# Half-by-half last units and a rearranged final LayerNorm in a two-block transformer kernel

## The chip, the cores and the metric

One core of a Trainium2 chip runs the whole program. The time is device microseconds of one execution, given as the median of several executions. The profile is one further execution, recorded by the hardware profiler; its times are counted from the start of its span.

## What is computed

The reference runs a token-mixing and feed-forward stack of two layers on a 512 x 1024 activation, and then one more block. That block ends with an expert layer, a residual and a LayerNorm, and only this end is touched here:

```python
x = layer_norm(DEEPNORM_ALPHA * x + f, ln2_g[l], ln2_b[l])      # f: the expert layer's output

def layer_norm(x, g, b):
    mu = jnp.mean(xf, axis=-1, keepdims=True)
    xc = xf - mu
    var = jnp.mean(xc * xc, axis=-1, keepdims=True)
    return xc * lax.rsqrt(var + LN_EPS) * g + b
```

The expert layer's second product is, over all 128 x 128 experts, (activation times gate) times the table v. For the last 384 of the 512 tokens it is done densely on TensorE, for the first 128 tokens by gathering the chosen rows of v.

## The kernel before, in words

The engines work as follows in the last stretch. A **unit** is one group of 128 experts: 128 x 1024 f32 numbers of v. `unit` (L253 to L262) loads it (DMA issued on SP, L257), rounds it to a high part `wh` on ScalarE (L260) and takes the rest `wl` on VectorE (L261); four raw buffers and three buffers each of `wh` and `wl` exist. `weighted` (L1884) also fetches the unit's activations, multiplies them by the gates (L1891) and splits them into `hi` and `lo` (`split`, L266 on ScalarE, L267 on VectorE). Products are made from high and low parts in three matmuls, (hi, wh), (lo, wh), (hi, wl), each into a PSUM bank of 128 tokens x 512 channels.

`second` (L1818) does this for one unit and one tile of 128 tokens `t`: three matmuls for each of the two channel halves m = 0 and 1, the halves in turn. There are three token tiles, so six PSUM banks `acc[2 * t + m]` sum up all units. For all units but the last five, `both` runs the three token tiles one after another, unit by unit: 18 matmuls a unit. The last five (`ENDS`) are held back as the list `ends`: the first two of them are split by halves into other buffers (`halves_in_blocks`), the other three use the three `wh` and `wl` buffers. They then run with the token tile as the outer loop, so that a tile's two banks are complete before the next tile begins: 30 matmuls a tile. After each tile `finish` is called.

`finish` (L1900) takes a tile of 128 tokens with 1024 channels. VectorE adds the residual, half by half, and sums each half (L1906); a one-column op makes minus the mean (L1909); ScalarE squares the row about the mean and sums it (L1911, with its accumulator read); VectorE makes the variance (L1912) and its reciprocal root by an integer estimate and three Newton steps (`rsqrt`, L325 to L331, nine one-column ops); one op makes mean times root (L1915). Then, for each half, ScalarE normalises (L1918), VectorE multiplies by the weight (L1919) and adds the bias (L1920), and SP issues the store (L1921). It is called four times: once for the gathered tile, ahead of `ends`, and once for each of the three dense tiles. Only its inputs differ.

**The order on each engine's queue** is not the order of the source. A planner of the framework goes through the program in its own estimated time and, each time an engine is free, takes the instruction that is ready and stands first in the source. An instruction whose input is not yet there lets one that stands later go ahead. Once planned, the order is fixed: on the chip each engine runs its queue in that order and waits where an input is late. The loads and splits of `ends` therefore stand among the instructions of the first `finish`.

Of the kernel before, what the change touches and what calls it, by code (L numbers as in the profile page):

```python
# [10 lines left out]
F32 = mybir.dt.float32  # L11
F32R = mybir.dt.float32r
BF = mybir.dt.bfloat16
I32 = mybir.dt.int32
U32 = mybir.dt.uint32
AF = mybir.ActivationFunctionType
OP = mybir.AluOpType
AX = mybir.AxisListType

P = 128  # L20
S = 512
D = 1024
# [8 lines left out]
LN_EPS = 1e-5  # L31
ALPHA = 2.0 ** 0.25
# [12 lines left out]
ROWS = 5  # L45
# [5 lines left out]
LEAD, ENDS = 7, 5  # L51
# [142 lines left out]
class Net:  # L194
# [1551 lines left out]
    def peer(self, out, begun):  # L1746
        nc, A = self.nc, self.A
        self.phase.close()
        self.stage = self.phase.enter_context(self.tc.tile_pool(name="stage", bufs=1))
        stage = self.stage  # L1750
# [12 lines left out]
        c0 = stage.tile([P, S], F32, name="c0", tag="c0")  # L1763
# [3 lines left out]
        XT = [self.cact] + [stage.tile([P, D], F32, name=f"xt{t}", tag=f"xt{t}") for t in range(1, NT)]  # L1767
        stats, heads = begun
        X, begun = [], [self.bank("proj") for _ in heads]
        for k, x in self.normed(stats, ln[:, 0], ln[:, 1], lambda k: self.x[k], self.t32):  # L1770
            X.append(self.new_pair())
            self.split(x, *X[k])
            c = slice(k * P, (k + 1) * P)
# [33 lines left out]
        def half(w, m):  # L1807
            return w[m] if isinstance(w, list) else w[:, m * S:(m + 1) * S]
# [6 lines left out]
                self.split(raw[:, m * S:(m + 1) * S], h[m], l[m])  # L1815
            return h, l

        def second(h, l, hi, lo, end, t):  # L1818
            for i, (a, w) in enumerate(((hi, h), (lo, h), (hi, l))):
                for m in range(2):  # L1820
                    q = 2 * t + m
                    nc.tensor.matmul(acc[q], lhsT=a[:, t * P:(t + 1) * P], rhs=half(w, m),  # L1822
                                     start=q not in started, stop=end and i == 2)
                    started.add(q)

        def both(args, end=False):
            for t in range(NT - early):
                second(*args, end, t)
# [23 lines left out]
        for j in range(kept, NE):  # L1852
# [6 lines left out]
            hi, lo = (v[:, :n] for v in self.new_pair())  # L1859
# [5 lines left out]
        row = [self.x[i] for i in range(4)]  # L1865
# [18 lines left out]
        def weighted(j, load=self.unit):  # L1884
            nonlocal fetched
            while fetched <= min(j + LEAD, 2 * j + 2):
                fetch(fetched)
                fetched += 1
            hs, g = coming.pop(0)
            w = load(A["pv"][:, j])  # L1890
            nc.vector.tensor_mul(hs, hs, g)  # L1891
            hi, lo = (v[:, :n] for v in self.new_pair())
            self.split(hs, hi, lo)
            return (*w, hi, lo)
# [4 lines left out]

        def finish(t, halves):  # L1900

            y = stage.tile([P, D], F32, name="row", tag="row", bufs=ROWS)
            parts, sq = self.sm(2, "fsum"), self.sm(2, "fsq")
            for m, v in enumerate(halves):
                c = slice(m * S, (m + 1) * S)
                nc.vector.scalar_tensor_tensor(y[:, c], XT[t][:, c], ALPHA, v, op0=OP.mult, op1=OP.add,  # L1906
                                               accum_out=parts[:, m:m + 1])
            mean, var = self.sm(1, "fmean"), self.sm(1, "fvar")
            nc.vector.scalar_tensor_tensor(mean, parts[:, :1], parts[:, 1:], self.negd, op0=OP.add, op1=OP.mult)  # L1909
            scr = stage.tile([P, D], F32, name="row", tag="row", bufs=ROWS)  # L1910
            nc.scalar.activation(scr, y, AF.Square, bias=mean, accum_out=sq[:, :1])  # L1911
            nc.vector.tensor_scalar(var, sq[:, :1], 1.0 / D, LN_EPS, op0=OP.mult, op1=OP.add)  # L1912
            r = self.rsqrt(var, 1)
            mr = self.sm(1, "fmr")
            nc.vector.tensor_mul(mr, mean, r)  # L1915
            for m in range(2):
                c = slice(m * S, (m + 1) * S)
                nc.scalar.activation(y[:, c], y[:, c], AF.Identity, scale=r, bias=mr)  # L1918
                nc.vector.tensor_mul(y[:, c], y[:, c], row[m])  # L1919
                nc.vector.tensor_add(y[:, c], y[:, c], row[2 + m])  # L1920
                nc.sync.dma_start(out[t * P:(t + 1) * P, c], y[:, c])  # L1921

        self.negd = self.sm(1, "negd", bufs=1)
        nc.vector.memset(self.negd, -1.0 / D)
        for j in range(kept - ENDS):
            both(weighted(j) if j else first)
            if not self.gathered:
                gather(ROW_STEPS[3])
                if self.gathered:
                    finish(0, [vacc[:, :S], vacc[:, S:]])  # L1930
        if not self.gathered:
            for _ in rows:
                pass
            finish(0, [vacc[:, :S], vacc[:, S:]])
        ends = [weighted(kept - ENDS + i, halves_in_blocks if i < ENDS - 3 else self.unit) for i in range(ENDS)]
        for t in range(NT - early):
            for i, e in enumerate(ends):
                second(*e, i == ENDS - 1, t)
            finish(early + t, acc[2 * t:2 * t + 2])


# [47 lines left out]
```

## Time and profile before

| what | us |
|---|---|
| median of 3 runs | 3672.79 |
| lowest and highest of them | 3670.61 and 3675.13 |
| the profiled execution, its own time | 3671.99 |
| the span of its profile | 3670.2 |

The span reaches from the first to the last instruction; the 1.8 us between it and the execution's own time lie around it. PE is TensorE's matmuls, PEld its weight loads, DVE is VectorE, ACT ScalarE, POOL GpSimd; SP issues DMAs. TensorE's granted clock is given as a share: 1.00 is 2.4 GHz, 0.50 is 1.2 GHz. A row of the timeline has start, duration, engine, line, operation, output and inputs, shapes and count; in brackets the idle time of the engine ahead of it and what ended that.

### The profile page before, as it was taken

The page shows a single profiled execution, that of the slowest core. Times are in us where ns is not written, and L with a number is a line of the kernel's source. Part 1 is how long each engine was busy: PE and PEld are TensorE (multiplying, and loading weights), DVE is VectorE, ACT ScalarE, POOL GpSimd, SP SyncE. Part 2 cuts the span into 40 slices and gives each one's busy share as a digit, 9 for nine tenths or more (in the row PEclk, how much of TensorE's full clock was granted, in tenths as well). Part 3 has the DMA queues.
Part 4 walks back from the last instruction along what each step waited for, and adds up shares of the span by engine and source line. Part 5 has one row for each costly group of instructions (what it writes and reads, how often), then busy time and mean ns, then how long its engine had stood idle before and what let it go on. Part 6 is the DMA issues. An engine that isn't in the chain of part 4 may idle for free. (4 is left out here: it accounts for less than half of the span.)

```text
span 3670.2 us, 49271 instructions
## 1 busy us (share of the span) xinstructions
PE 3554.5 (97%) x18265; PEld 3019.0 (82%) x18265; DVE 2394.7 (65%) x4791; ACT 1562.9 (43%) x2769; POOL 369.2 (10%) x358
## 2 busy tenths in 40 slices
PE   7999999999999999999999999899899999999998
PEld 6888876788888888767888887788899999988786
DVE  6555687665563334776533386699877667778787
ACT  4332366433233323465432263433667753334333
POOL 0000100000000001000000000021221134432220
PEclk9999999999999999999999999999999999999999
DMA  7666320266653333401333322265686879999995
GB/s 249 190 186 198 115 94 18 64 202 193 201 178 109 94 95 105 133 24 31 91 98 93 97 79 68 84 202 195 206 289 235 296 262 308 313 327 346 336 341 183
DMA packets 259665, 635.72 MB, mean 173 GB/s; under 512 B 82336, under 2 KB 117584, under 8 KB 256864
## 3 DMA queue, kind: packets, MB, share of 16 engines
q1 hardware_dynamic: 206368, 473.96, 40.1%
q0 software_dynamic: 39808, 140.52, 11.2%
q10 hardware_dynamic: 13248, 18.09, 1.3%
q8 instruction: 143, 2.34, 0.3%
q14 instruction: 98, 0.80, 0.1%
HBM read 591.32 MB, written 41.16 MB: 172 GB/s over the span
## 5 line engine op out<-in xcount | busy, mean ns | idle before, releaser
L260 ACT ACTIVATE wh<-raw 128x1024 fp32r<-128x1024 f32 (+2 forms) x620 | 645.3, 1043 | 1129.3 <-PE proj L283 880.6
L261 DVE TENSOR_TENSOR wl<-raw,wh 128x1024 fp32r<-128x1024 f32 (+2 forms) x620 | 744.1, 1201 | 508.4 <-ACT wh L260 370.1
L283 PE MATMUL proj<-yh,wh 128*128 128x512 f32 (+1 forms) x2744 | 644.7, 375 | 9.1 <-ACT hg L1839 4.2
L283 PE MATMUL proj<-yh,wl 128*128 128x512 f32 (+1 forms) x2744 | 629.1, 371 | 13.6 <-DVE wl L261 13.6
L283 PE MATMUL proj<-yl,wh 128*128 128x512 f32 (+1 forms) x2744 | 628.4, 370 | 0.0
L283 PEld LDWEIGHTS proj<-yh,wl 128*128 128x128 f32 x2744 | 506.4, 189 | 82.8 <-DVE wl L261 15.5
L283 PEld LDWEIGHTS proj<-yh,wh 128*128 128x128 f32 x2744 | 501.1, 189 | 85.0 <-ACT hg L1839 5.7
L283 PEld LDWEIGHTS proj<-yl,wh 128*128 128x128 f32 x2744 | 505.4, 189 | 67.5
L535 DVE SCALAR_TENSOR_TENSOR scr<-raw,cact 128x1024 bf16<-128x1024 f32 x128 | 156.7, 1224 | 136.3 <-DMA raw<-in_wada 136.0
L1822 PE MATMUL acc<-wl,yh 128*128 128x512 f32 x756 | 236.2, 394 | 2.7 <-DVE wl L261 2.6
L1822 PE MATMUL acc<-wh,yh 128*128 128x512 f32 x756 | 235.0, 392 | 3.6 <-ACT yh L266 2.1
L1822 PE MATMUL acc<-wh,yl 128*128 128x512 f32 x756 | 234.3, 391 | 0.3 <-DVE yl L267 0.3
L1737 POOL DMA_INDIRECT row<-in_purows,c x128 | 156.5, 1223 | 537.9 <-DVE row L1721 261.6
L667 DVE TENSOR_TENSOR ga<-sg,proj 128x512 f32<-128x512 f32 x88 | 60.5, 687 | 225.7 <-PE proj L283 223.2
L1737 POOL DMA_INDIRECT row<-in_pv,c x128 | 165.2, 1291 | 392.6 <-DVE vacc L1729 275.8
L272 PE MATMUL proj<-yl,wh 128*128 128x256 f32 (+1 forms) x552 | 177.0, 330 | 10.6 <-DVE yl L394 7.0
L273 PE MATMUL proj<-yh,wl 128*128 128x256 f32 (+1 forms) x552 | 174.6, 324 | 2.2 <-DVE wl L261 2.2
L1822 PEld LDWEIGHTS acc<-wl,yh 128*128 128x128 f32 x756 | 141.1, 188 | 38.4 <-DVE wl L261 9.5
L271 PE MATMUL proj<-yh,wh 128*128 128x256 f32 (+1 forms) x552 | 164.8, 328 | 7.8 <-ACT yh L640 6.3
L1822 PEld LDWEIGHTS acc<-wh,yh 128*128 128x128 f32 x756 | 142.1, 189 | 32.0 <-ACT yh L266 2.5
L1822 PEld LDWEIGHTS acc<-wh,yl 128*128 128x128 f32 x756 | 142.5, 189 | 31.4 <-DVE yl L267 1.0
L1729 DVE SCALAR_TENSOR_TENSOR vacc<-row,act,vacc 128x1024 f32<-128x1024 f32 x127 | 162.5, 1280 | 0.6
(465 smaller groups left out, 5166.7 us busy)
## 6 DMA issues: line engine op xcount, KB each, us to landing
raw<-in_wada SPq DMA_DIRECT2D x144, 512.0 KB
raw<-in_pu SPq DMA_DIRECT2D x128, 512.0 KB
raw<-in_pv SPq DMA_DIRECT2D x128, 512.0 KB
raw<-in_wg SPq DMA_DIRECT2D x84, 512.0 KB
raw<-in_wu SPq DMA_DIRECT2D x84, 512.0 KB
raw<-in_wd SPq DMA_DIRECT2D x64, 512.0 KB
gates<-st SPq DMA_DIRECT2D x20, 1024.0 KB
acts<-hg ACTq DMA_DIRECT2D x92, 192.0 KB
```

The source lines that it names most:

```text
L260: nc.scalar.activation(h[:, :n], raw[:, :n], AF.Copy)
L261: self.latest = nc.vector.tensor_sub(l[:, :n], raw[:, :n], h[:, :n].bitcast(F32)).ins
L271: mm(out, lhsT=lh, rhs=rh, start=start, stop=False)
L272: mm(out, lhsT=lh, rhs=rl, start=False, stop=False)
L273: mm(out, lhsT=ll, rhs=rh, start=False, stop=stop)
L283: self.nc.tensor.matmul(ps, lhsT=w[:, k * P:(k + 1) * P], rhs=X[c + k][part], start=c + k + i == 0, stop=i == 2 and c + k == nk - 1)
L535: nc.vector.scalar_tensor_tensor(scr, raw, 1.0, self.cact, op0=OP.mult, op1=OP.mult, accum_out=self.mod[:, l, j:j + 1])
L667: nc.vector.tensor_mul(a, sg, p[1])
L1729: nc.vector.scalar_tensor_tensor(acc, row, a, acc, op0=OP.mult, op1=OP.add)
L1737: nc.gpsimd.indirect_dma_start(out=row, out_offset=None, in_=tables[kind], in_offset=bass.IndirectOffsetOnAxis(ap=self.experts[:GT, s:s + ...
L1822: nc.tensor.matmul(acc[q], lhsT=a[:, t * P:(t + 1) * P], rhs=half(w, m), start=q not in started, stop=end and i == 2)
```

## The change

In the loop over the last five units the channel half becomes an outer loop: for each token tile first all five units for half 0 (15 matmuls), then all five for half 1. `second` gets the halves as an argument; `both` still runs both.

In `finish`, each half of the row is squared by itself as soon as it is there, about minus the mean of the first half (`c0`), with a bf16 scratch as the output that is not used. The difference `off` between the full mean and `c0` corrects the variance afterwards. VectorE subtracts the mean and multiplies by the weight into a second row buffer `z`, ahead of the root; after the root one op for each half multiplies by the root and adds the bias. ScalarE's normalising pass and the product of mean and root are gone. The stores are as before.

```diff
--- before.py
+++ after.py
@@ -1815,9 +1815,9 @@
                 self.split(raw[:, m * S:(m + 1) * S], h[m], l[m])
             return h, l
 
-        def second(h, l, hi, lo, end, t):
+        def second(h, l, hi, lo, end, t, halves=range(2)):
             for i, (a, w) in enumerate(((hi, h), (lo, h), (hi, l))):
-                for m in range(2):
+                for m in halves:
                     q = 2 * t + m
                     nc.tensor.matmul(acc[q], lhsT=a[:, t * P:(t + 1) * P], rhs=half(w, m),
                                      start=q not in started, stop=end and i == 2)
@@ -1899,26 +1899,31 @@
 
         def finish(t, halves):
 
+
             y = stage.tile([P, D], F32, name="row", tag="row", bufs=ROWS)
+            z = stage.tile([P, D], F32, name="row", tag="row", bufs=ROWS)
+            scr = self.tmp.tile([P, D], BF, name="scr", tag="scr", bufs=1)
             parts, sq = self.sm(2, "fsum"), self.sm(2, "fsq")
+            c0, mean, var, off = (self.sm(1, v) for v in ("fc0", "fmean", "fvar", "foff"))
+            cs = [slice(m * S, (m + 1) * S) for m in range(2)]
             for m, v in enumerate(halves):
-                c = slice(m * S, (m + 1) * S)
-                nc.vector.scalar_tensor_tensor(y[:, c], XT[t][:, c], ALPHA, v, op0=OP.mult, op1=OP.add,
+                nc.vector.scalar_tensor_tensor(y[:, cs[m]], XT[t][:, cs[m]], ALPHA, v, op0=OP.mult, op1=OP.add,
                                                accum_out=parts[:, m:m + 1])
-            mean, var = self.sm(1, "fmean"), self.sm(1, "fvar")
+                if m == 0:
+                    nc.vector.tensor_scalar(c0, parts[:, :1], -1.0 / S, None, op0=OP.mult)
+                nc.scalar.activation(scr[:, cs[m]], y[:, cs[m]], AF.Square, bias=c0, accum_out=sq[:, m:m + 1])
+
             nc.vector.scalar_tensor_tensor(mean, parts[:, :1], parts[:, 1:], self.negd, op0=OP.add, op1=OP.mult)
-            scr = stage.tile([P, D], F32, name="row", tag="row", bufs=ROWS)
-            nc.scalar.activation(scr, y, AF.Square, bias=mean, accum_out=sq[:, :1])
-            nc.vector.tensor_scalar(var, sq[:, :1], 1.0 / D, LN_EPS, op0=OP.mult, op1=OP.add)
+            nc.vector.tensor_scalar(off, mean, c0, None, op0=OP.subtract)
+            for m in range(2):
+                nc.vector.scalar_tensor_tensor(z[:, cs[m]], y[:, cs[m]], mean, row[m], op0=OP.add, op1=OP.mult)
+            nc.vector.tensor_scalar(off, off, off, -LN_EPS, op0=OP.mult, op1=OP.add)
+            nc.vector.tensor_scalar(var, sq[:, :1], sq[:, 1:], 1.0 / D, op0=OP.add, op1=OP.mult)
+            nc.vector.tensor_scalar(var, var, off, None, op0=OP.subtract)
             r = self.rsqrt(var, 1)
-            mr = self.sm(1, "fmr")
-            nc.vector.tensor_mul(mr, mean, r)
             for m in range(2):
-                c = slice(m * S, (m + 1) * S)
-                nc.scalar.activation(y[:, c], y[:, c], AF.Identity, scale=r, bias=mr)
-                nc.vector.tensor_mul(y[:, c], y[:, c], row[m])
-                nc.vector.tensor_add(y[:, c], y[:, c], row[2 + m])
-                nc.sync.dma_start(out[t * P:(t + 1) * P, c], y[:, c])
+                nc.vector.scalar_tensor_tensor(z[:, cs[m]], z[:, cs[m]], r, row[2 + m], op0=OP.mult, op1=OP.add)
+                nc.sync.dma_start(out[t * P:(t + 1) * P, cs[m]], z[:, cs[m]])
 
         self.negd = self.sm(1, "negd", bufs=1)
         nc.vector.memset(self.negd, -1.0 / D)
@@ -1934,8 +1939,9 @@
             finish(0, [vacc[:, :S], vacc[:, S:]])
         ends = [weighted(kept - ENDS + i, halves_in_blocks if i < ENDS - 3 else self.unit) for i in range(ENDS)]
         for t in range(NT - early):
-            for i, e in enumerate(ends):
-                second(*e, i == ENDS - 1, t)
+            for m in range(2):
+                for i, e in enumerate(ends):
+                    second(*e, i == ENDS - 1, t, [m])
             finish(early + t, acc[2 * t:2 * t + 2])
```

## Rows read from the trace of the kernel before

**Rows 1.** The page, part 1: busy time and share of the span, by engine.

```profile
PE 3554.5 (97%) x18265; PEld 3019.0 (82%) x18265; DVE 2394.7 (65%) x4791; ACT 1562.9 (43%) x2769; POOL 369.2 (10%) x358
```

**Rows 2.** The chain of work that ended last: start, us, what; its last piece.

```profile
3666.42 0.69 DVE row L1920
```

**Rows 3.** Busy time by stretch: tiles 1, 2, 3, and the end (clock, DMA share last).

```profile
3632.58:3641.77 9.19, 7.38 (x31) 5.47 (x30) 7.80 (x20) 4.47 (x7) 0.00 (x0) 1.00 0.07 29
3641.77:3648.59 6.82, 6.82 (x31) 5.63 (x30) 4.22 (x17) 2.67 (x4) 0.00 (x0) 1.00 0.10 38
3648.59:3655.60 7.01, 6.96 (x31) 5.44 (x29) 5.35 (x19) 1.33 (x3) 0.00 (x0) 1.00 0.19 75
3655.60:3670.20 14.60, 0.00 (x0) 0.00 (x0) 8.86 (x26) 4.28 (x6) 0.00 (x0) 0.64 0.19 72
```

**Rows 4.** Timeline of VectorE over the last tile's `finish`.

```profile
3655.83 0.69 DVE L1906 SCALAR_TENSOR_TENSOR row<-xt,acc 128x512 f32<-128x512 f32 x1
...
3656.44 0.68 DVE L1906 SCALAR_TENSOR_TENSOR row<-xt,acc 128x512 f32<-128x512 f32 x1
...
3657.05 1.29 DVE L1919 TENSOR_TENSOR row<-row,x 128x512 f32<-128x512 f32 x2
...
3659.46 0.21 DVE L1909 SCALAR_TENSOR_TENSOR fmean<-fsum,negd 128x1 f32<-128x1 f32 x1
3660.98 0.15 DVE L1912 TENSOR_SCALAR fvar<-fsq 128x1 f32<-128x1 f32 x1 [1.31 <-ACT row L1911]
3661.17 0.15 DVE L325 TENSOR_SCALAR rsg<-fvar 128x1 int32<-128x1 int32 x1
...
3663.28 0.16 DVE L1915 TENSOR_TENSOR fmr<-fmean,rsy 128x1 f32<-128x1 f32 x1
3664.37 0.69 DVE L1919 TENSOR_TENSOR row<-row,x 128x512 f32<-128x512 f32 x1 [0.93 <-ACT row L1918]
```

**Rows 5.** Timeline around the last units: VectorE, then ScalarE, then TensorE.

```profile
3629.97 0.69 DVE L1906 SCALAR_TENSOR_TENSOR row<-cact,vacc 128x512 f32<-128x512 f32 x1
...
3631.86 1.21 DVE L267 TENSOR_TENSOR yl<-hs,yh 128x384 fp32r<-128x384 f32 x2
...
3634.66 1.22 DVE L261 TENSOR_TENSOR wl<-raw,wh 128x1024 fp32r<-128x1024 f32 x1
...
3639.33 0.69 DVE L1919 TENSOR_TENSOR row<-row,x 128x512 f32<-128x512 f32 x1
3639.93 1.22 DVE L261 TENSOR_TENSOR wl<-raw,wh 128x1024 fp32r<-128x1024 f32 x1
...
3633.54 1.04 ACT L260 ACTIVATE wh<-raw 128x1024 fp32r<-128x1024 f32 x1
3637.14 1.52 ACT L1918 ACTIVATE row<-row,fmr,rsy 128x512 f32<-128x512 f32 x2 [2.56 <-issue]
3638.57 1.04 ACT L260 ACTIVATE wh<-raw 128x1024 fp32r<-128x1024 f32 x1
...
3639.66 0.74 PE L1822 MATMUL acc<-wh,yh 128*128 128x512 f32 x2 [1.49 <-ACT wh L260]
...
3641.20 0.73 PE L1822 MATMUL acc<-wl,yh 128*128 128x512 f32 x2 [0.33 <-DVE wl L261]
```

**Rows 6.** Groups by line and shape over the whole span: two kinds of VectorE op.

```profile
L1161 DVE SCALAR_TENSOR_TENSOR p<-p,w 128x512 f32<-128x512 f32 x8 | 6.0, 745 | 0.0
...
L330 DVE TENSOR_SCALAR rst<-rsy,fvar 128x1 f32<-128x1 f32 x12 | 3.3, 272 | 0.4
```

**Rows 7.** Busy time by stretch, columns as in rows 3: clock around earlier TensorE gaps.

```profile
2932.44:2934.46 2.02, 0.01 (x2) 0.01 (x1) 1.81 (x4) 1.56 (x4) 1.34 (x1) 1.00 0.70 251
...
2935.93:2939.34 3.41, 3.41 (x12) 3.41 (x11) 2.25 (x4) 3.23 (x9) 1.14 (x1) 0.50 0.96 338
...
2594.61:2604.85 10.24, 9.03 (x27) 8.53 (x28) 10.24 (x58) 3.09 (x4) 2.34 (x2) 0.50 0.66 206
```

## Prediction

> **What bounds the kernel now.** I read the page first: TensorE is busy 97% of the span, VectorE 65% [rows 1]. So only what makes TensorE wait, or what comes after its last matmul, can show. The change touches nothing ahead of the first `finish` and the last five units, about the last 41 us of 3670. Next I read the chain that ended last: it is `finish` of the last tile [rows 2]. Then the stretches [rows 3]: each begins with a tile's first matmul. Tile 2 is 30 matmuls in 6.82 us, 0.227 us each, with the PE column full; tile 1 takes 9.19 us, so TensorE waits about 2.4 us in it or at its edges; after 3655.60 there are 14.60 us without a matmul. These two, the wait in tile 1 and the tail, are what the change can move. 0.2% of this time is 7.3 us, which is about what a measurement of this kernel can tell from no change.
>
> **The tail, and VectorE's work per tile.** From the last tile's second L1906 (3656.44) to the last L1920's end (3666.42 + 0.69 = 3667.11) pass 10.7 us [rows 2, 4]. Three parts of that are not needed: 2.4 us (3657.05 to 3659.46) in which VectorE still finishes the tile before, 1.31 us of waiting for the full-row square, and 1.1 us from the product of mean and root (3663.28) to the first L1919 (3664.37), ScalarE's normalising pass [rows 4]. Both ScalarE round trips leave the chain.
>
> VectorE pays for it. Before, a tile costs it two L1906 at 0.61, L1909 0.25, L1912 0.19, the root 2.1 (3661.17 to 3663.28), the product 0.2 and four row ops at 0.61 to 0.67: 6.6 us [rows 4]. After: two L1906 1.2; `c0` 0.2; the mean 0.25; `off` 0.25; two products (y + mean) * weight; the correction 0.2; two variance ops 0.5; the root 2.1; two ops that scale and add the bias. The four row ops now take a column as scalar; the nearest such row, L1161, takes 0.745 us against 0.69 [rows 4, 6], so I take a pitch of 0.67, 2.7 us for four. Sum **7.4 us a tile**. The five new one-column ops aren't in the trace. They lie between a pitch of 0.07, as if fully overlapped, and 0.3 for a Newton step's op with two column scalars (0.272 busy, L330 [rows 6]); I take 0.2 to 0.25 as most of them have one such operand. The ends give 6.8 and 7.8 us a tile.
>
> 7.4 is more than the 6.82 us in which TensorE makes a tile, so VectorE sets the pace of the last three tiles. Let T be the end of tile 1's matmuls. Its second half is taken up some 0.3 us later (L1906 follows the last matmul by at most that [rows 3, 4]). What is left of tile 1 is 7.4 less a first L1906 and `c0`: 6.6. Two more tiles are 14.8. The end is T + 0.3 + 6.6 + 14.8 = T + 21.7. Before, T is 3641.77 and the end 3667.11: T + 25.3. **The tail gives 3.6 us.** The first half's early sum and square (ScalarE, two half rows and two reads instead of one row and one) are covered by the row products; a full-row square and read make VectorE wait 1.31 [rows 4], so this is the cost of a half at most, were that cover gone. The first `finish` works on gathered rows alone and gains nothing by halves, but it gets the same longer VectorE list. The last stores still take 3.1 us from 3667.11 to the span's end; their issue moves from 1.3 us apart to 0.7, worth nothing to 0.6 us later, and I take nothing.
>
> **The wait for the last unit.** This decides the sign. Before, tile 1 runs 24 matmuls, both halves of four units, before it asks for the fifth unit; there it waits 1.49 us for `wh` and 0.33 us for `wl` [rows 5]. That `wh` stands on ScalarE behind the two L1918 of the first `finish` (3637.14), which wait for its root. Those leave the queue, so `wh` can follow the one at 3633.54 and be done by about 3635.6. But `wl` is VectorE's, and there L261 stands behind the same `finish` (3639.33, then 3639.93). After the change, half 0 asks for the last unit after only 12 matmuls. Tile 1 begins at 3632.58, so this is 3635.3, and `wl` is wanted two matmuls later, at 3635.8.
>
> Where will L261 stand? The planner prefers what stands first in the source. `finish` comes first; L261 only slips into a gap where a one-column op waits for the one before. One of the two splits sits in such a gap (3634.66), the last one (3639.93) came only behind the root and most row ops [rows 5]. I take the same for after. The queue from 3629.97 on is: L1906 0.7, `c0` 0.2, L261 1.2, mean 0.2, two L267 1.2, `off` 0.2, two products 1.3, three one-column ops 0.7, L267 0.5, L261 1.2, root 2.1, two last row ops 1.3, and then the last L261 1.2: 12.0 us, so `wl` is there at **3642.0** (3641.2 before). TensorE then still owes 16 matmuls of tile 1 instead of two: 3.6 us, T = 3645.6, **3.9 us later** (3641.77 before).
>
> With L261 ahead of the two last row ops it would be 2.5 later. The other bound is L261 straight behind its `wh`, 3635.6 + 1.2 = 3636.8: a wait of 1.0, and T = 3632.58 + 6.82 + 1.0 = 3640.4, 1.3 us earlier than before.
>
> **The clock.** A wait of about 6 us (3635.8 to 3642.0, less a few matmuls) is longer than any TensorE had in this stretch. Its clock stayed at 1.00 over the 1.5 us wait [rows 3, 5]. Elsewhere, after a gap of 2.0 us, the granted clock stood at 0.50, which is 1.2 GHz, for the next 3.41 us; the longest such stretch that I read, 10.24 us, followed a longer gap [rows 7]. At 0.50 half of the stretch is lost. Nothing to 5.1 us are the bounds; I take one short stretch, **1.7 us**, as part of it can fall into the wait itself.
>
> **Sum:** 3.9 + 1.7 - 3.6 = +2.0 us on the profiled execution's 3671.99, which is 3674.0. That execution lies 0.8 under the median of the runs; the runs spread over 4.5 us, so I leave it there. It is no measurable change.
>
> VectorE is at 65% of the span and at 4.22 of 6.82 us in tile 2 [rows 1, 3], so it looks far from full. The Trainium skill says in "Perfetto Trace Analysis", Optimizing Scalar/DVE Operations, that where these engines aren't saturated but cause bubbles elsewhere, breaking up instructions may let work complete sooner. By that rule TensorE's pace would hold; my row-by-row sum says that the change itself fills VectorE. The rule's case is the second rival.
>
> **The rivals.**
> - The planner puts the last L261 early (into a gap of the root, say). For it: one split sits in such a gap, and ScalarE is free sooner. Against: the last unit's buffers come free late, and `finish` got longer on VectorE. With the early bound, -1.3 - 3.6 = -4.9: 3667.1, no clock loss. In between, L261 ahead of the last two row ops: 2.5 + 1.0 - 3.6, about 3672.
> - VectorE keeps up, and the tiles run at TensorE's pace. The end is T + 13.6 + 0.3 + 6.6 = T + 20.5, 1.1 us sooner than I say: 3672.9. It needs under 6.8 us a tile, the low end above.
> - Slower: the wait at the last unit drops the clock for long. With 10.24 us at half, 3.9 + 5.1 - 3.6 = +5.4: 3677.4. It would pass 0.2% from a half-clock stretch of 14 us on, and no row shows one with TensorE at work. If the clock stayed low over all 76 matmuls left, that is the case.
> - The halves do nothing: VectorE is behind anyway when half 0 is complete, so its early sum buys no time. This is within my sum, as VectorE sets the pace there.
>
> **Chances.** My forecast 0.5 (3671 to 3677); early L261 0.25; TensorE's pace 0.15; long half clock 0.1, a half of it beyond 0.2%. A gain of over 7.3 us needs the early split, TensorE's pace and more at once: 0.05. So faster 0.05, same 0.89, slower 0.06. The range reaches from the early split's 3667.0 to the long half clock's 3677.5.
>
> **What would show it.** Right: in tile 1 a TensorE wait on L261 of 3 us or more, after 12 to 15 matmuls; a clock of 0.50 behind it; VectorE without gaps from tile 1's end on; the end some 21.7 us after tile 1's. Wrong: the last L261 ahead of the root's end, tile 1 in under 9 us, or VectorE idle ahead of the last tile's second L1906.

## The result, and the profile after

The changed kernel takes **3716.37 us** (median of 5 runs, 3712.79 to 3728.95) against 3673.16 (5 runs) before: ratio **1.0122** with a 95% interval of 1.0104 to 1.0140. The forecast was 3674.0 and no measurable change; the kernel is 43 us slower than before. The profiled execution is the slowest of the five, 3728.95, with a span of 3727.1, so its times lie 57 us over before's span rather than 43.

First the page of the changed kernel: the span and part 1, to be read against [rows 1].

```profile
span 3727.1 us, 49271 instructions
...
PE 3613.8 (97%) x18265; PEld 3027.7 (81%) x18265; DVE 2396.4 (64%) x4803; ACT 1559.4 (42%) x2769; POOL 370.5 (10%) x358
```

TensorE runs the same 18265 matmuls and is still busy 97% of the span, but 59.3 us longer in sum (3613.8 against 3554.5). This is a little more than the difference of the spans (56.9). The time went into the matmuls themselves, not into waits.

Next, where in the span it went. The first matmul of the last five units is a fixed event: the change has no instruction of TensorE ahead of it. It starts at 3632.58 before [rows 3] and at 3689.52 after, 56.9 us later. From there to the end of the span pass 37.6 us before (3670.20 - 3632.58) and 37.6 us after (3727.10 - 3689.52). **All of the loss arises ahead of the code that was changed.** With the n-th matmul of one trace beside the n-th of the other, the lag is 3 us at 186 us, 14 at 860, 30 at 1450 and 47 at 2400. It is still 47 at 3000, and 57 from 3450 on. So it does not arise at one place: it grows where matmuls of 512 columns run (750 to 900 us hold 662 of them and add 4.4 us, 0.0066 each) and stands still where there are few (340 of the 3373 matmuls from 2400 to 3000).

Then one stretch in the middle. The timeline of TensorE of the kernel before, 800 to 806 us; a row is a run of matmuls with its start and duration:

```profile
800.57 1.98 PE L283 MATMUL proj<-yh,wh 128*128 128x512 f32 x8
802.38 1.98 PE L283 MATMUL proj<-yl,wh 128*128 128x512 f32 x8
804.20 1.98 PE L283 MATMUL proj<-yh,wl 128*128 128x512 f32 x8
```

and the same of the changed kernel:

```profile
800.08 2.03 PE L283 MATMUL proj<-yh,wl 128*128 128x512 f32 x8
801.95 2.03 PE L283 MATMUL proj<-yh,wh 128*128 128x512 f32 x8
803.82 2.03 PE L283 MATMUL proj<-yl,wh 128*128 128x512 f32 x8
```

From start to start, eight matmuls take 1.815 us before (half of 804.20 - 800.57) and 1.87 after: a pitch of 0.227 and of 0.234 us. No row has a wait in brackets. The same comes out of windows over 60 us (window, us, PE busy and count, granted clock, DMA share, GB/s), first of the kernel before, then of the changed one:

```profile
800.00:860.00 60.00, 60.00 (x267) 1.00 0.63 196
```

```profile
800.00:860.00 60.00, 60.00 (x259) 1.00 0.63 190
```

TensorE has no gap and its clock is at 1.00, which is 2.4 GHz, but it makes 259 matmuls in a time in which the kernel before makes 267. Neither a late input nor the clock explains that: the same instruction is 3% slower. Lines L283 and L1822 alone have 7008 and 2304 matmuls of 512 columns; 9312 times 0.0066 us would be 61 us. Not all of that shows: from 3450 to 3600 us 642 of them run and the lag does not grow. There the kernel before itself waits 1.7 us for inputs, with a DMA share of 1.01.

**The last 38 us went much as forecast.** The stretches of the changed kernel, tiles 1, 2, 3 and the end (columns as in [rows 3]), and, as the last row, the stretch behind tile 1's wait:

```profile
3689.52:3703.30 13.78, 9.89 (x31) 7.24 (x30) 8.17 (x23) 2.61 (x5) 0.00 (x0) 0.75 0.11 39
3703.30:3710.26 6.96, 6.96 (x31) 5.63 (x30) 6.41 (x23) 1.63 (x4) 0.00 (x0) 1.00 0.00 0
3710.26:3717.40 7.14, 7.12 (x31) 5.45 (x29) 6.79 (x24) 1.63 (x4) 0.00 (x0) 1.00 0.20 75
3717.40:3727.10 9.70, 0.00 (x0) 0.00 (x0) 6.19 (x21) 0.81 (x2) 0.00 (x0) 0.60 0.29 108
...
3697.15:3702.00 4.85, 4.85 (x11) 3.79 (x12) 0.85 (x3) 0.81 (x2) 0.00 (x0) 0.50 0.09 32
```

Tile 1 takes 13.78 us instead of 9.19, and the end without matmuls 9.70 instead of 14.60. TensorE's timeline has the wait in brackets:

```profile
3692.79 0.47 PE L1822 MATMUL acc<-wh,yl 128*128 128x512 f32 x1
3697.15 0.80 PE L1822 MATMUL acc<-wl,yh 128*128 128x512 f32 x1 [3.88 <-DVE wl L261]
3697.74 0.63 PE L1822 MATMUL acc<-yh 128*128 128x512 f32 x1
```

After 14 matmuls TensorE waits 3.88 us for the last `wl`, and comes back at a granted clock of 0.50. VectorE's timeline says why, and what pace the tiles have:

```profile
3690.12 0.21 DVE L1920 TENSOR_SCALAR foff<-foff 128x1 f32<-128x1 f32 x1
3690.25 0.20 DVE L1921 TENSOR_SCALAR fvar<-fsq 128x1 f32<-128x1 f32 x1
...
3694.54 1.41 DVE L1925 SCALAR_TENSOR_TENSOR row<-row,rsy,x 128x512 f32<-128x512 f32 x2
3695.87 1.22 DVE L261 TENSOR_TENSOR wl<-raw,wh 128x1024 fp32r<-128x1024 f32 x1
...
3703.50 0.69 DVE L1910 SCALAR_TENSOR_TENSOR row<-xt,acc 128x512 f32<-128x512 f32 x1 [4.64 <-PE acc L1822]
...
3710.47 0.68 DVE L1910 SCALAR_TENSOR_TENSOR row<-xt,acc 128x512 f32<-128x512 f32 x1
...
3717.44 0.68 DVE L1910 SCALAR_TENSOR_TENSOR row<-xt,acc 128x512 f32<-128x512 f32 x1
...
3722.60 1.42 DVE L1925 SCALAR_TENSOR_TENSOR row<-row,rsy,x 128x512 f32<-128x512 f32 x2
```

The last split stands behind the root and both last row ops (L1925) of the first `finish`, and each tile's second half (L1910, before L1906) follows the one before by 6.97 us. The first two rows are new one-column ops; they start 0.13 us apart.

### The profile page after: what moved, and what is told of

Read it like the earlier page. It is cut to its first block, busy times and chain, and to the rows that moved or that the text cites. A ratio compares the mean times of both kernels' runs of the same rounds, so it can differ in the third digit from the quotient of the medians.

```text
span 3727.1 us, 49271 instructions
## 1 busy us (share of the span) xinstructions
PE 3613.8 (97%) x18265; PEld 3027.7 (81%) x18265; DVE 2396.4 (64%) x4803; ACT 1559.4 (42%) x2769; POOL 370.5 (10%) x358
## 4 chain that ended last, share of the span: by engine, by line
PE 82%; DVE 11%; DMA 3%; ACT 2%; issue 1%; SPq 0%; ACTq 0%; DVEq 0%
PE proj L283 52%; PE acc L1822 13%; PE proj L272 2%; PE proj L273 2%; PE proj L271 2%; DVE wl L261 2%; PE gp L1690 2%; PE o L1091 1%; PE tp L869 1%; PE sc L809 1%; DMA gates<-st 1%; PE pnat L271 1%; PE pnat L272 1%; PE pnat L273 1%; DVE ch L1343 1%
## 5 line engine op out<-in xcount | busy, mean ns | idle before, releaser
L261 DVE TENSOR_TENSOR wl<-raw,wh 128x1024 fp32r<-128x1024 f32 (+2 forms) x620 | 744.1, 1201 | 549.1 <-ACT wh L260 419.2
L283 PE MATMUL proj<-yh,wh 128*128 128x512 f32 (+1 forms) x2744 | 653.6, 378 | 8.5 <-ACT hg L1839 4.0
L283 PE MATMUL proj<-yh,wl 128*128 128x512 f32 (+1 forms) x2744 | 641.3, 376 | 12.6 <-DVE wl L261 12.6
L283 PE MATMUL proj<-yl,wh 128*128 128x512 f32 (+1 forms) x2744 | 640.3, 375 | 0.0
L283 PEld LDWEIGHTS proj<-yh,wl 128*128 128x128 f32 x2744 | 507.6, 189 | 92.4 <-DVE wl L261 14.8
L283 PEld LDWEIGHTS proj<-yh,wh 128*128 128x128 f32 x2744 | 500.5, 189 | 93.9 <-ACT hg L1839 5.5
L283 PEld LDWEIGHTS proj<-yl,wh 128*128 128x128 f32 x2744 | 506.9, 189 | 77.6
L1822 PE MATMUL acc<-wl,yh 128*128 128x512 f32 x756 | 239.8, 397 | 3.9 <-DVE wl L261 3.9
L1822 PE MATMUL acc<-wh,yl 128*128 128x512 f32 x756 | 239.5, 396 | 4.1 <-DVE yl L267 4.1
L1822 PE MATMUL acc<-wh,yh 128*128 128x512 f32 x756 | 239.4, 396 | 2.9 <-ACT yh L266 2.9
L1822 PEld LDWEIGHTS acc<-wh,yl 128*128 128x128 f32 x756 | 142.9, 189 | 39.0 <-DVE yl L267 4.7
L1822 PEld LDWEIGHTS acc<-wl,yh 128*128 128x128 f32 x756 | 142.8, 189 | 39.0 <-DVE wl L261 5.3
L1822 PEld LDWEIGHTS acc<-wh,yh 128*128 128x128 f32 x756 | 142.0, 189 | 34.0 <-ACT yh L266 3.3
```

The costliest lines, as they stand in the source:

```text
L261: self.latest = nc.vector.tensor_sub(l[:, :n], raw[:, :n], h[:, :n].bitcast(F32)).ins
L283: self.nc.tensor.matmul(ps, lhsT=w[:, k * P:(k + 1) * P], rhs=X[c + k][part], start=c + k + i == 0, stop=i == 2 and c + k == nk - 1)
```

## The experiments

**The question.** The change has no instruction ahead of its last 41 us that differs, yet matmuls of 512 columns are slower all over the span. What it can change far from its code is where buffers lie. Its one-column tiles come from the pool `small`: `fc0` and `foff` are new there and `fmr` is gone. In the built program each one-column tile takes 32 bytes of a partition and each name has four buffers, so the pool grows by 128 bytes. The large buffers allocated behind it (activations, rows, stage) move from 103936 to 104064; the units' buffers, allocated ahead of it (raw 41472, `wh` 57856, `wl` 70144), stay. Before, all these distances are multiples of 512 bytes. Among the kernel's filling tiles, which are never read, are 120 columns of f32 ahead of the units' buffers (L521) and `PAD = 40` columns in `small` (L53, L522). With them one can move these buffers without another edit. In a matmul one operand is loaded into the array, 128 x 128, and the other streams past it, 512 columns. At L1822 the activations are loaded and `wh` or `wl` streams; at L283 it is the other way round. Either way one operand is an activation and the other a part of a unit (but for two of the last five units, whose parts lie among the activations).

The table gives what all but the last run measured, so that the texts below need not repeat it. The tail is the time from the first matmul of the last five units to the end of the span, each from its own trace; in the six traces of before's own code, its own and those of e2 and e5 to e8, it came out between 35.3 and 38.7.

| run | median, us | before beside it | ratio, 95% | tail, us |
|---|---|---|---|---|
| e1_after_realigned | 3673.15 | 3675.64 | 0.9992 (0.9981 to 1.0003) | 38.2 |
| e2_before_moved_128B | 3720.79 | 3675.64 | 1.0114 (1.0098 to 1.0130) | 37.2 |
| e3_halves_only | 3677.46 | 3675.64 | 1.0007 (0.9996 to 1.0018) | 40.3 |
| e4_norm_only_realigned | 3668.16 | 3675.64 | 0.9979 (0.9969 to 0.9990) | 32.8 |
| e5_before_all_moved_128B | 3676.61 | 3674.14 | 1.0004 (0.9993 to 1.0015) | 38.7 |
| e6_before_weights_moved_128B | 3719.13 | 3674.14 | 1.0126 (1.0109 to 1.0143) | 35.3 |
| e7_before_moved_256B | 3673.29 | 3674.14 | 1.0004 (0.9992 to 1.0015) | 37.4 |
| e8_before_moved_32B | 3720.66 | 3674.14 | 1.0130 (1.0112 to 1.0149) | 35.4 |
| e9_after_last_units_first | 3674.19 | 3673.62 | 1.0005 (0.9996 to 1.0014) | 38.0 |
| e10_short_norm | 3668.84 | 3673.62 | 0.9989 (0.9980 to 0.9998) | 31.5 |
| e11_short_norm_units_first | 3669.10 | 3673.62 | 0.9984 (0.9975 to 0.9994) | 31.9 |
| e12_short_norm_units_first_halves | 3668.56 | 3673.62 | 0.9990 (0.9977 to 1.0003) | 31.5 |

**Is it the placement?** The changed kernel with the filling tile shortened by what `small` has grown:

```diff
-PAD = 40
+PAD = 8
```

> The change whole, with the padding column tile shortened from 40 to 8 numbers (128 bytes), so that all large buffers behind it lie again where they lay before the change; nothing else differs. Placement theory (the 128 bytes by which the change's small tiles moved the large buffers make every 512-column matmul some 3% slower): about 3673 us, within 0.15% of before; the 512-column matmul pitch in the feed-forward stages is back from 0.233 to 0.227 us. Code theory (the new order of the last units or the new norm slows the kernel by itself): 3716 us, as the change.

The slowdown is gone. The same window of this kernel:

```profile
800.00:860.00 60.00, 60.00 (x267) 1.00 0.62 194
```

It has before's 267 matmuls. The other way round, the kernel **before** with `PAD = 72`, so that only the 128 bytes of the change are left of it:

> The kernel before, with the padding column tile lengthened from 40 to 72 numbers (128 bytes), so that the large buffers lie where the change has them; not one instruction else differs. Placement theory: 3710 to 3725 us, 1.0 to 1.4% slower than before. Code theory: 3673 us, no change.

```profile
800.00:860.00 60.00, 60.00 (x259) 1.00 0.59 187
```

It has the changed kernel's 259. No instruction differs from before but in its addresses, and one memset in its size, and the ratio is 1.0114. The two runs together carry the whole result: the slowdown is the placement, and what the change does apart from it cannot be told from nothing (0.9992, interval 0.9981 to 1.0003).

**Place or distance?** First the units' buffers and everything allocated behind them moved by 128 bytes together:

```diff
-        self.pad(c, "pad2", 120)
+        self.pad(c, "pad2", 152)
```

> The kernel before with the constants' padding tile 128 bytes longer: the weight buffers (raw, high, low part) and the large activation buffers all lie 128 bytes further on, so their distance to one another stays. Theory 'distance' (the weight read and the activation read of a matmul get in each other's way when they don't lie alike): no change, 3673 to 3676 us, feed-forward pitch 0.227 us. Theory 'place' (a row of 512 numbers must begin at a multiple of 512 bytes by itself): as slow as the change or slower, 3715 to 3760 us, pitch 0.233 us or more.

Then the same edit with `PAD = 8`, which moves the units' buffers (and the temporary tiles right behind them) and leaves the activations where they were:

> The kernel before with 128 bytes more ahead of the weight buffers and 128 fewer behind them: weights (and the small temporary tiles) move by 128 bytes, the large activation buffers stay. Theory 'distance': slow as the run with the activations moved, 3715 to 3725 us. Theory 'place': slow too, as the weights are one operand of every large matmul. Theory 'activations only' (only these buffers matter, whatever operand they are): no change, 3673 to 3676 us.

The window of e5, then that of e6:

```profile
800.00:860.00 60.00, 60.00 (x266) 1.00 0.61 194
```

```profile
800.00:860.00 60.00, 60.00 (x260) 1.00 0.61 189
```

Moved together they cost nothing (1.0004); moved without the activations, the units cost what the activations cost (1.0126 against 1.0114). So it is the distance between the two, not the place of either.

**Which distances?** The kernel before with `PAD = 104` (256 bytes more) and with `PAD = 48` (32 bytes more):

> The kernel before with the large activation buffers 256 bytes further on, weights unmoved. If multiples of 256 bytes are enough: 3673 to 3676 us and a pitch of 0.227 us. If only multiples of 512 do, or the distance to the weights counts in full: 3700 us or more.

> The kernel before with the large activation buffers 32 bytes further on, the smallest step that the allocation has; weights unmoved. If any step off the old place costs the same: 3715 to 3725 us. If the cost grows with the distance: 3680 to 3695 us. If it is a matter of 64 or 128 bytes only: 3673 to 3676 us.

The window of e7, then that of e8:

```profile
800.00:860.00 60.00, 60.00 (x267) 1.00 0.62 198
```

```profile
800.00:860.00 60.00, 60.00 (x259) 1.00 0.62 190
```

256 bytes cost nothing and 32 bytes the full price. This kernel has no room for a shift by 512 bytes.

**Whose reads collide?** In the kernel all engines read those buffers at once. This kernel, of which there is one execution, leaves the whole network out and copies its input to the output; it has 96 f32r matmuls of 512 columns for each of several distances, with eight stationary blocks in turn (`w`) and one streamed operand (`mv`). In L33 to L41 only the column at which `mv` is read differs (0, 8, 16, 24, 32, 48, 64, 96 and 128 columns of 4 bytes), in L42 both operands are 128 bytes on, in L43 only `w`; L50 and L56 are as L33, with ScalarE copying beside them:

```diff
+        run(lambda k: mm(ps[k % 2], lhsT=w[:, k % 8 * P:(k % 8 + 1) * P], rhs=mv[:, 0:0 + S], start=True, stop=True))
+        run(lambda k: mm(ps[k % 2], lhsT=w[:, k % 8 * P:(k % 8 + 1) * P], rhs=mv[:, 8:8 + S], start=True, stop=True))
...
+        run(lambda k: mm(ps[k % 2], lhsT=w[:, 32 + k % 7 * P:32 + (k % 7 + 1) * P], rhs=mv[:, 32:32 + S], start=True, stop=True))
+        run(lambda k: mm(ps[k % 2], lhsT=w[:, 32 + k % 7 * P:32 + (k % 7 + 1) * P], rhs=mv[:, 0:S], start=True, stop=True))
```

> Not the network: the input is copied to the output, and beside it eleven groups of 96 matmuls (128x128 weights, 512 columns, the type of the kernel's) run with nothing else on the core, the activations 0, 32, 64, 96, 128, 192, 256, 384 and 512 bytes off the weights' place, then both 128 bytes on, then the weights alone 128 bytes on; at the end two groups with distance 0 while ScalarE copies 1024 columns at distance 0 and at 128 bytes. If TensorE's own two reads are what collides: a pitch of 0.227 us at 0, 256 and 512 bytes and with both moved, 0.230 to 0.240 us at the other distances, without any other engine. If it is another engine beside TensorE: 0.227 us or less in all the first eleven groups, and more in the last one.

TensorE's timeline of this run (start, us; the pitch is from one start to the next, over 96), and a window over most of it:

```profile
10.40 24.17 PE L33 MATMUL ps<-mv,w 128*128 128x512 f32 x96 [10.40 <-ACT mv L24]
34.40 22.57 PE L34 MATMUL ps<-mv,w 128*128 128x512 f32 x96
56.81 22.15 PE L35 MATMUL ps<-mv,w 128*128 128x512 f32 x96
78.79 22.57 PE L36 MATMUL ps<-mv,w 128*128 128x512 f32 x96
101.20 22.56 PE L37 MATMUL ps<-mv,w 128*128 128x512 f32 x96
123.60 22.56 PE L38 MATMUL ps<-mv,w 128*128 128x512 f32 x96
146.00 21.94 PE L39 MATMUL ps<-mv,w 128*128 128x512 f32 x96
167.78 22.55 PE L40 MATMUL ps<-mv,w 128*128 128x512 f32 x96
190.17 21.94 PE L41 MATMUL ps<-mv,w 128*128 128x512 f32 x96
211.95 21.93 PE L42 MATMUL ps<-mv,w 128*128 128x512 f32 x96
233.71 22.55 PE L43 MATMUL ps<-mv,w 128*128 128x512 f32 x96
256.11 21.96 PE L50 MATMUL pt<-mv,w 128*128 128x512 f32 x96
277.90 21.92 PE L56 MATMUL pu<-mv,w 128*128 128x512 f32 x96
```

```profile
34.00:250.00 216.00, 216.00 (x937) 175.66 (x936) 0.00 (x0) 0.00 (x0) 0.00 (x0) 1.00 0.00 1
```

The window shows that from L34 to L43 nothing but TensorE runs, at full clock: VectorE, ScalarE, GpSimd and the DMAs are at 0.00. Still a group takes 22.4 us at 32, 96, 128, 192 and 384 bytes (L34, L36 to L38, L40) and with `w` alone moved (L43): a pitch of 0.2332 to 0.2334. It takes 21.8 at 256 and 512 bytes and with both moved, which is distance 0 (L39, L41, L42): 0.2267 to 0.2269. At 64 bytes (L35) it is 21.98, a pitch of 0.2290. L33 as a whole is no reading of distance 0, as it began at a lower clock; L50, at distance 0 with ScalarE beside it, is (277.90 - 256.11 = 21.79). These two pitches are those of the kernels after and before. So TensorE alone makes the difference: no other engine reads that memory, and the pitch of its matmuls depends on how far apart its stationary blocks and its streamed operand lie. It was lowest at 0, 256 and 512 bytes. That its two reads get in each other's way at the other distances is the plainest reading; where they meet is not shown.

**The parts of the change by themselves.** The halves alone (the new loop and argument of `second`, the old `finish`, `PAD = 40`, nothing new in `small`):

> Only the half-by-half order of the last five units; the norm is that of before, the buffers lie where they lay. My stretch-by-stretch sum: TensorE asks for the last unit after 12 matmuls, the last split of VectorE still stands behind the first norm's root and row ops; a wait of some 4 us, a stretch at half clock, and nothing back in the tail but the early half: 3675 to 3680 us, slower by 2 to 7. Rival (the halves bring tile results sooner and the wait is hidden): 3670 to 3672.

```profile
3641.00 0.68 PE L1822 MATMUL acc<-wh,yh 128*128 128x512 f32 x1 [3.24 <-ACT wh L260]
```

The tail is 40.3, 2.8 us longer than before's; the medians do not tell the two kernels apart (1.0007). Asking for the last unit after 12 matmuls costs a wait of 3.24 us, here for `wh`, which still stands behind ScalarE's two L1918.

The new `finish` alone, with the old loop and `PAD = 8`:

> Only the rearranged norm, old order of the last units, buffers back where they lay. Sum: the tail loses two ScalarE round trips, the wait for the last unit stays near 1.8 us as there are 24 matmuls to run ahead of it: 3 to 6 us faster than before, 3667 to 3670. Rival (VectorE's longer list per tile sets the pace and eats it): 3672 to 3674.

Its wait on TensorE, then (second fence) the first op of each of the three tiles on VectorE:

```profile
3643.82 0.72 PE L1822 MATMUL acc<-wl,yh 128*128 128x512 f32 x2 [1.34 <-DVE wl L261]
```

```profile
3644.36 0.69 DVE L1910 SCALAR_TENSOR_TENSOR row<-xt,acc 128x512 f32<-128x512 f32 x1 [0.59 <-PE acc L1822]
...
3651.46 0.68 DVE L1910 SCALAR_TENSOR_TENSOR row<-xt,acc 128x512 f32<-128x512 f32 x1
...
3658.57 0.68 DVE L1910 SCALAR_TENSOR_TENSOR row<-xt,acc 128x512 f32<-128x512 f32 x1
```

The tail is 32.8, 4.8 us shorter, and the kernel is faster than before (0.9979). VectorE takes 7.10 us a tile without a gap, more than TensorE's 6.82 [rows 3], so it sets the pace. The parts make -4.8 and +2.8, and both together, realigned, +0.6 (e1): 2.6 us more than their sum. These are single traces, and the medians are too coarse to confirm the 2.6. In the traces the difference lies in tile 1, which takes 0.8 us less than before in e4, 3.5 more in e3 and 5.3 more in e1. Behind tile 1 the parts add up: counted from its end, the last VectorE op ends 4.0, 0.8 and 4.6 us earlier. In the old loop the longer list of VectorE delays the last `wl` where only two matmuls are left of tile 1, and the wait is 1.34 us; with the halves outside it meets the 15th matmul, and the wait is 3.89 us with the half clock behind it.

**Can the wait go?** If the order of the source put the last split behind `finish`, `finish(0)` written behind `ends` would let it go ahead:

```diff
-                if self.gathered:
-                    finish(0, [vacc[:, :S], vacc[:, S:]])
-        if not self.gathered:
-            for _ in rows:
-                pass
-            finish(0, [vacc[:, :S], vacc[:, S:]])
+        for _ in rows:
+            pass
         ends = [weighted(kept - ENDS + i, halves_in_blocks if i < ENDS - 3 else self.unit) for i in range(ENDS)]
+        finish(0, [vacc[:, :S], vacc[:, S:]])
```

> The change realigned (padding 8), with the last five units prepared ahead of the first norm in the source, so that VectorE splits the last unit ahead of that norm's ops. If the wait for the last unit (3.89 us in the realigned change, and the half clock behind it) stands there only because of that order: the wait is under 0.6 us, no half-clock stretch, and the stretch from the last units' first matmul to the end of the span shrinks from 38.2 to 32 to 34 us; 3667 to 3670 us in all. Rival (VectorE's 7 us a tile set the end whatever comes before): 36 us or more, 3672.

This missed. TensorE's wait, then VectorE's last split:

```profile
3642.13 0.80 PE L1822 MATMUL acc<-wl,yh 128*128 128x512 f32 x1 [2.95 <-DVE wl L261]
```

```profile
3640.86 1.22 DVE L261 TENSOR_TENSOR wl<-raw,wh 128x1024 fp32r<-128x1024 f32 x1
3641.99 0.75 DVE L1925 SCALAR_TENSOR_TENSOR row<-row,rsy,x 128x512 f32<-128x512 f32 x1
```

The split passes one of the two last row ops and no more, and the wait falls from 3.89 (e1) to 2.95; it still stands behind the whole root. So its place in the source is not the main thing that holds it back. That it becomes ready that late in the planner's own time, because its buffers come free late, fits this, but was only argued.

**A shorter finish.** The product ahead of the root as in the change, but with one square over the full row about the full mean, so without `c0`, `off` and the correction; the old loop, and `PAD = 72` to keep the distance:

```diff
...
             nc.scalar.activation(scr, y, AF.Square, bias=mean, accum_out=sq[:, :1])
+            for m in range(2):
+                nc.vector.scalar_tensor_tensor(z[:, cs[m]], y[:, cs[m]], mean, row[m], op0=OP.add, op1=OP.mult)
...
```

> The old order of the last units and the weight's product ahead of the root, but the square about the full mean, in one pass, so that the four correction ops of one column go; buffers kept in place (padding 72). VectorE's work a tile is then 6.4 us by the rows, under TensorE's 6.82. If VectorE's pace set the end in the norm-only run (32.8 us from the last units' first matmul): about 31 us here, 3666 us. Rival (the full-row square stands in the way, as the product covers only 1.3 of its 1.4 us): 32.8 us or more, no better than the norm-only run.

Again the first op of each tile on VectorE:

```profile
3642.19 0.69 DVE L1909 SCALAR_TENSOR_TENSOR row<-xt,acc 128x512 f32<-128x512 f32 x1 [0.60 <-PE acc L1822]
...
3649.05 0.69 DVE L1909 SCALAR_TENSOR_TENSOR row<-xt,acc 128x512 f32<-128x512 f32 x1 [0.21 <-PE acc L1822]
...
3655.85 0.69 DVE L1909 SCALAR_TENSOR_TENSOR row<-xt,acc 128x512 f32<-128x512 f32 x1 [0.15 <-PE acc L1822]
```

Now VectorE waits for TensorE in every tile, 6.86 and 6.80 us apart, and the tail is 31.5. Two more put `finish(0)` behind `ends` as in e9, and the second of them also runs tiles 2 and 3 half by half:

> The same with the last five units prepared ahead of the first norm. No wait left in the last units: 20.5 us of matmuls, 6.9 for the last norm and 3.1 for the store: 30.5 us from the last units' first matmul, 3664 to 3666 us, 0.2% faster than before. Rival (nothing left to gain): as the run before it.

> The same, with the second and third of the dense tiles half by half: the last tile's first half is added up while TensorE works on the second, 0.6 us less in the tail: 29.9 us, 3664 to 3666. Rival (VectorE is behind and cannot use it): no difference to the run before.

Neither gains anything on e10 that can be told (tails of 31.9 and 31.5); in e11 the wait for the last split, which was expected to go, is 1.46 us against 1.12 in e10. e4, e10 and e11 are 0.1 to 0.2% faster than the kernel before, and e12 cannot be told from it; between the four the intervals overlap.

## Why the prediction was wrong

- **The step that failed** is the premise ahead of the sum: "The change touches nothing ahead of the first `finish` and the last five units, about the last 41 us of 3670". Its instructions touch nothing there; its memory does. The new one-column tiles were priced as VectorE ops and never as bytes, and no rival had a price on what lies where. Every duration ahead of the last 41 us was taken over as fixed, and L283's 0.227 us was not: 0.0066 us more for each of 9312 matmuls would be 61 us, of which 57 show in the trace and 43 in the medians. No row of the kernel before shows such a cost, since there all distances were multiples of 512 bytes; but the filling tiles stood in the code, and the diff of the names in `small` could have been added up against them. The signs that the prediction named as right (a wait of 3 us or more after 12 to 15 matmuls, a clock of 0.50 behind it, VectorE without gaps from there) came true, and the end came 20.7 us after tile 1's, for the 21.7 that it named. They look at the last 41 us alone and could not show this step wrong.
- The Trainium skill says in "SBUF — State Buffer", Who interferes with whom, that TensorE has two read ports, one for the streamed operand and one for loading weights, independent of each other. By that one would expect the distance to cost nothing. The run of matmuls alone differs (0.2334 against 0.2267 us), and the measurement decides.
- **The wait for the last unit** was right in kind and place: the last L261 behind the root and both row ops, a wait after 14 matmuls, 3.88 us long. The clock of 0.50 followed it. With T the end of tile 1, counted from its start, T came 4.6 us later than before (13.78 against 9.19), and 5.3 later in e1, without the slower pitch, where the forecast had 3.9 + 1.7 = 5.6. That this is near is partly luck. VectorE's list up to the last split was put at 12.0 us and took 10.8 (from the second L1910, at 3686.27, to 3695.87 + 1.22 = 3697.09), which is the larger part of why the wait was 3.88 and not about 6. The half clock took more than its 1.7: the 16 matmuls behind the wait took 6.15 us (3703.30 - 3697.15), and 6.31 in e1, where 16 at 0.227 take 3.6. The rival of an early split did not occur.
- **The tail.** The last VectorE op ends at 3722.60 + 1.42 = 3724.02, T + 20.7, where the forecast had T + 21.7 and before T + 25.3: it gives 4.6, not 3.6. The term that was mis-sized is VectorE's work per tile: 6.97 us in the changed kernel and also 6.97 in e1, and 7.10 in e4, instead of 7.4. The new one-column ops were priced at 0.2 to 0.25 us; those shown above start 0.13 apart, and the list ahead of the wait was put too long in part for the same reason. In e1 TensorE's tile 2 takes 6.82, so VectorE does set the pace, by 0.15 us and not by 0.6. What the prediction drew from the Trainium skill's "Perfetto Trace Analysis", Optimizing Scalar/DVE Operations, that with the work broken up TensorE's pace would hold, was thus not borne out, though nearly; e10, with less work for VectorE, is where TensorE's pace holds.
- **The sum** of these parts was +2.0; the tail measured 0.0 in the changed kernel and +0.6 realigned. As the effect of the change apart from the placement the forecast holds (e1: 3673.15, no measurable change), with the offsetting errors just named in it.
- **The halves do nothing** was nearly right, and understates it: behind T they bring 0.6 us (the last VectorE op ends at T + 20.72 in e1 and T + 21.36 in e4), but ahead of T they cost 6.0 (tile 1 takes 14.45 us in e1 and 8.41 in e4). These are single traces.

## What to carry to other kernels

A change's cost is also the bytes it adds: small tiles in a pool ahead of large buffers move those, and the table of addresses should be compared before the instructions are. Keep the two operands of a matmul at a distance that is a multiple of 256 bytes (shown for 512 columns of f32r, at 0, 256 and 512 bytes and the larger multiples of this kernel); and where many stages are slower by a like share with no wait and a full clock, compare the pitch of one unchanged instruction and suspect the placement. The effect of a local change is then read from a fixed event to the end of the span, not from the total.

## What of the hardware was not expected

The speed of an f32r matmul of 512 columns depends on how far apart its two operands lie in a partition: 0.2267 to 0.2269 us at 0, 256 and 512 bytes, 0.2332 to 0.2334 at 32, 96, 128, 192 and 384 bytes, 0.2290 at 64, with no other engine at work. As little as 32 bytes cost the full 3%, and moving both operands together costs nothing. In the whole kernel that is 1.1 to 1.3%, for two reasons. The 9312 matmuls of L283 and L1822 fill 2114 of 3670 us (9312 times 0.227). And part of the loss falls where TensorE would wait anyway: in e6 and e8 tile 1 runs without a wait, in 6.94 and 6.95 us instead of 9.19, and their tails are 2 us shorter than before's. What in the memory collides is not shown by any run here.
